# Input projection of a gated convolution block: thirteen seven-product duals and four plain gate blocks in place of twelve duals and eight plain blocks

## The chip, the cores and the metric

The kernel runs on one core of one Trainium2 chip. The core has a matrix engine (TensorE, "PE" in the profile), VectorE (DVE), ScalarE (ACT), GpSimd (POOL), SyncE (SP, which here only issues transfers) and 16 DMA engines. Each engine works through its own list of instructions in order and waits on semaphores for the others. The metric is device time of one execution in microseconds (us).

## The reference

One layer over a sequence of 1024 positions with 1024 channels, in float32 (here cut to the mixing half):

```
h    = rms_norm(x, norm_mix_g) * (1 + sc1) + sh1          # sc1, sh1 from silu(c) @ w_ada + b_ada
proj = h @ w_in                                           # 1024 -> 7 * 1024
b_s, c_s, v_s, v_c, gl_c, gate_a, gate_b = split(proj)
y_a  = (b_s * causal_dwconv3(c_s * v_s)) @ w_short_out
u    = causal_dwconv31(v_c * sigmoid(gl_c)) + bias
y_b  = silu(layer_norm(u)) @ w_conf_out
x    = x + g1 * ((sigmoid(gate_a) * y_a + sigmoid(gate_b) * y_b) @ w_o)
```

Behind it come a second norm, a SwiGLU of width 2816 and a final norm. The change is in `proj = h @ w_in` alone.

## The kernel before

**Layout and precision.** Activations lie transposed: 128 channels on the partitions, positions along the free axis, in two halves of 512. The 1024 channels of h are eight chunks, k = 0 to 7. w_in has 56 output blocks of 128 channels. Each float32 product is made of three matmuls on rounded operands (`mm3`, lines 380 to 383): weights high times x high, weights high times x low, weights low times x high. `split_w` makes the two weight parts: a cast on ScalarE (`wh`, line 226) and a difference on VectorE or GpSimd (`wl`, line 227). There are five raw weight buffers (`raw`), three `wh` and three `wl`; a raw buffer is free for the next load once its split or its matmul is through, and a `wl` once its product is.

**The stages.** The projection runs in three parts.

1. *The lead* (`row_blocks`, called twice): seven blocks at once, one PSUM bank each, chunk by chunk, first for the first half of the positions, then for the second. The activations come to be during it: for each chunk of the first half VectorE reduces two loads of w_ada against silu(c) (`modulation`, line 361), scales x (line 462), splits the weights, and with ScalarE makes the high and low part of h (`modulate`, lines 470 and 471). The first three chunks use whole float32 weights (line 376). In chunk 6 TensorE also sums the squares of the second half (`sum_x1`), from which its norm follows. The seven blocks are three pairs (gl, v) for the long convolution, whose gated product u VectorE makes at the end (`glu`, line 560), and one gate block.
2. *A plain block* (`col_block`): one gate block, both halves, 48 matmuls.
3. *Twelve duals.* A dual takes four output blocks as two pairs, and the matrix of 2 x 2 (upper and lower four chunks by first and second half of the positions) is multiplied with seven products instead of eight, in the order `PRODUCTS = "1265734"`. A product is two pairs times four chunks times three matmuls: 24. The sums of activations that products 6, 5, 7 and 4 need are made once, in VectorE, after the lead. The sums of weights are made per dual on GpSimd (`dual_units`, lines 246 to 251 and 293), which makes `wl` for the duals too. Product 1 goes to bank x, which ScalarE copies to bank y; product 2 is added to y, and 6, 7 and 4 to x; 5 and 3 go to bank z. `win_evac` takes each result out.

**What sets the order.** The program is written in one order, and a planner then lays out each engine's list, by its own estimate of durations and by when a buffer comes free; `tc.issue_after` pins some instructions behind others. `next_w` keeps weights two products ahead. Beside the duals VectorE works off the 31-tap convolution in 46 taps for each channel block (line 915); `CONV_DUALS` spreads the eight blocks over the first eleven duals, each tap pinned behind an evacuation (`read_at`).

## Time and profile before

| | us |
|---|---|
| median of 3 runs (lowest, highest) | 1471.91 (1470.99, 1473.99) |
| the profiled execution | 1470.4 |
| its span, first to last instruction | 1468.6 |
| TensorE busy, share of the span | 1457.7, 99% |
| VectorE busy | 1179.1, 80% |
| ScalarE busy | 615.4, 42% |
| GpSimd busy | 515.8, 35% |

In the rows that follow the first two numbers of a timeline row are the start and the length in us; then come engine, source line, operation, what is written and read, the shape, the count, and in brackets the idle time before and what ended it. "L381" is line 381 of the kernel before. A busy matmul overlaps the next one, so the pace of TensorE is read from the distance of starts. The lead runs from 16.15 to about 97 us, the plain block to about 108, the duals to about 565.

### The profile page before, as it was taken

The page shows a single profiled execution, that of the slowest core. Times are in us where ns is not written, and L with a number is a line of the kernel's source. Part 1 is how long each engine was busy: PE and PEld are TensorE (multiplying, and loading weights), DVE is VectorE, ACT ScalarE, POOL GpSimd, SP SyncE. Part 2 cuts the span into 40 slices and gives each one's busy share as a digit, 9 for nine tenths or more (in the row PEclk, how much of TensorE's full clock was granted, in tenths as well). Part 3 has the DMA queues.
Part 4 walks back from the last instruction along what each step waited for, and adds up shares of the span by engine and source line. Part 5 has one row for each costly group of instructions (what it writes and reads, how often), then busy time and mean ns, then how long its engine had stood idle before and what let it go on. Part 6 is the DMA issues. An engine that isn't in the chain of part 4 may idle for free.

```text
span 1468.6 us, 17760 instructions
## 1 busy us (share of the span) xinstructions
PE 1457.7 (99%) x6443; PEld 1197.3 (82%) x6443; DVE 1179.1 (80%) x1627; ACT 615.4 (42%) x895; POOL 515.8 (35%) x464
## 2 busy tenths in 40 slices
PE   9999999999999999999999999999999999999997
PEld 5888888888888888888888888888888888888887
DVE  8999898887998969999688799776777665676755
ACT  4753333333433346455235475343444443222325
POOL 0046677767777771111022002110111015435005
PEclk9999999999999999999999999999999999999999
DMA  9412313222322258375586337655554449988403
GB/s 369 177 52 72 101 60 127 72 86 101 101 70 76 95 205 300 115 251 206 195 313 219 105 109 236 227 172 166 178 170 170 149 155 373 345 285 275 144 15 115
DMA packets 83913, 247.97 MB, mean 169 GB/s; under 512 B 9665, under 2 KB 11713, under 8 KB 83826
## 3 DMA queue, kind: packets, MB, share of 16 engines
q1 hardware_dynamic: 43072, 138.63, 27.5%
q0 software_dynamic: 37008, 95.63, 19.6%
q10 hardware_dynamic: 3746, 12.59, 2.3%
q8 instruction: 50, 0.82, 0.2%
q14 instruction: 37, 0.30, 0.1%
HBM read 184.41 MB, written 62.39 MB: 168 GB/s over the span
## 4 chain that ended last, share of the span: by engine, by line
PE 97%; DVE 1%; POOL 0%; issue 0%; ACT 0%; POOLq 0%; DVEq 0%
PE bank L380 12%; PE bank L383 12%; PE bank L381 12%; PE x L381 8%; PE x L383 8%; PE x L380 8%; PE z L381 4%; PE z L380 4%; PE z L383 4%; PE y L380 3%; PE y L381 3%; PE y L383 3%; PE mix L383 2%; PE yb L383 2%; PE yb L380 2%; PE mix L381 2%
## 5 line engine op out<-in xcount | busy, mean ns | idle before, releaser
L226 ACT CAST wh<-raw 128x1024 fp32r<-128x1024 f32 (+2 forms) x253 | 255.6, 1011 | 467.6 <-PE bank L381 126.8
L227 POOL TENSOR_TENSOR wl<-raw,wh 128x1024 fp32r<-128x1024 f32 x84 | 204.8, 2446 | 82.1 <-ACT wh L226 82.1
L227 DVE TENSOR_TENSOR wl<-raw,wh 128x1024 fp32r<-128x1024 f32 (+2 forms) x169 | 193.7, 1146 | 37.9 <-ACT wh L226 36.7
L915 DVE SCALAR_TENSOR_TENSOR c<-diff,vec,c 128x512 f32<-128x512 f32 x232 | 171.0, 753 | 4.4
L1263 POOL DMA_DIRECT2D hid<-stage x71 | 37.9, 534 | 346.0 <-DVE stage L421 341.5
L380 PE MATMUL bank<-th,wh 128*128 128x512 f32 x288 | 112.0, 389 | 0.0
L381 PE MATMUL bank<-tl,wh 128*128 128x512 f32 x288 | 112.0, 389 | 0.0
L383 PE MATMUL bank<-th,wl 128*128 128x512 f32 x288 | 112.0, 389 | 0.0
L915 DVE SCALAR_TENSOR_TENSOR c<-u,wsum,c 128x512 f32<-128x512 f32 x112 | 84.3, 753 | 2.6
L246 POOL TENSOR_TENSOR raw<-raw 128x1024 f32<-128x1024 f32 x12 | 29.2, 2431 | 124.1 <-DVE wl L227 86.9
L420 ACT CAST stage<-g 128x512 fp32r<-128x512 f32 x62 | 38.4, 622 | 72.8 <-DMA hid<-stage 39.6
L421 DVE TENSOR_TENSOR stage<-g,stage 128x512 fp32r<-128x512 f32 x62 | 42.5, 689 | 27.5 <-ACT stage L420 27.4
L383 PEld LDWEIGHTS bank<-th,wl 128*128 128x128 f32 x288 | 54.1, 188 | 11.3
L381 PEld LDWEIGHTS bank<-tl,wh 128*128 128x128 f32 x288 | 54.1, 188 | 11.2
L380 PEld LDWEIGHTS bank<-th,wh 128*128 128x128 f32 x288 | 54.1, 188 | 11.2
L1289 POOL DMA_DIRECT2D th<-hid x71 | 38.1, 537 | 53.6 <-PE x L383 32.7
L380 PE MATMUL x<-th,wh 128*128 128x512 f32 x144 | 56.1, 390 | 0.1
L383 PE MATMUL x<-th,wl 128*128 128x512 f32 x144 | 56.0, 389 | 0.0
L381 PE MATMUL x<-tl,wh 128*128 128x512 f32 x144 | 56.0, 389 | 0.0
L246 DVE TENSOR_TENSOR raw<-raw 128x1024 f32<-128x1024 f32 (+1 forms) x17 | 19.2, 1130 | 40.1 <-DMA raw<-in_w_fi 29.0
L380 PE MATMUL yb<-zsh,wh 128*128 128x512 f32 x128 | 49.8, 389 | 0.0
L381 PE MATMUL yb<-zsl,wh 128*128 128x512 f32 x128 | 49.8, 389 | 0.0
(812 smaller groups left out, 4243.2 us busy)
## 6 DMA issues: line engine op xcount, KB each, us to landing
hid<-stage POOLq DMA_DIRECT2D x71, 512.0 KB, 4.6
raw<-in_w_fi SPq DMA_DIRECT2D x54, 512.0 KB, 4.5
raw<-in_w_duals SPq DMA_DIRECT2D x48, 512.0 KB, 3.5
th<-hid POOLq DMA_DIRECT2D x71, 256.0 KB, 5.6
tl<-hid POOLq DMA_DIRECT2D x71, 256.0 KB, 5.6
ada<-in_ada SPq DMA_DIRECT2D x24, 512.0 KB, 5.9
raw<-in_ada SPq DMA_DIRECT2D x24, 512.0 KB, 4.8
raw<-in_w_fo SPq DMA_DIRECT2D x24, 384.0 KB, 5.8
```

Of the source, the lines that this page charges most:

```text
L226: hi = nc.scalar.copy(wh, raw)
L227: lo = lo_engine.tensor_tensor(wl, raw, f32(wh), ALU.subtract)
L246: eng.tensor_tensor(a["s1"], a["21"], a["22"], ALU.add)
L380: nc.tensor.matmul(ps, wh, xh, start=first, stop=False, skip_group_check=again)
L381: nc.tensor.matmul(ps, wh, xl, start=False, stop=False, skip_group_check=again)
L383: mm3.ins = nc.tensor.matmul(ps, wl, xh, start=False, stop=last, skip_group_check=again).ins
L420: t_split.act = nc.scalar.copy(hi, src).ins
L421: t_split.ins = nc.vector.tensor_tensor(lo, src, f32(hi), ALU.subtract).ins
L915: tap.ins = nc.vector.scalar_tensor_tensor(out=out, in0=src[:, s : s + H], scalar=wt, in1=acc, op0=ALU.mult, op1=ALU.add).ins
L1263: nc.gpsimd.dma_start(hid_dram[key], s)
L1289: nc.gpsimd.dma_start(t, hid_dram[key][:, s])
```

## The change

- The lead's seven blocks are now three gate blocks and the four blocks of the two first duals (v and gl of u0 and u1, c and v of p0 and p1). For the latter the lead's first half makes products 1 and 2 of both duals: after four chunks the bank holds product 1, ScalarE copies it to SBUF (`half_way`, into `m1`), and the other four chunks add product 2 to the same bank. The second half makes only the three gate blocks, with splits of 384 columns in place of 896.
- The plain block is the fourth gate block. There are 26 pairs, so thirteen duals; the GLU is made by `win_evac` in all eight cases, and `glu` goes.
- After the plain block come products 1 and 2 of dual 2, then the other five products of duals 0, 1 and 2, then ten duals of seven products (`win_order`). For duals 0 and 1 ScalarE copies product 1 from `m1` into bank x before product 6.
- Duals 0 to 2 use `apart_units`, which loads a block when a product needs it (a second load of block 22 in each). VectorE makes the splits of products 1 and 2 of dual 2 and all of product 6 of dual 0, two sums and a split; GpSimd the rest.
- The sums of activations for products 7 and 4 move behind the plain block in the text. The taps are spread from dual 1.0 over 11.2 duals. `CLOCK` has four filling matmuls in place of five in one place.

```diff
 LEAD = 7
+GATES = 3
+BEGUN = 2
-CLOCK = (10, 3, (5,), 9, 5)
+CLOCK = (10, 3, (5,), 9, 4)
...
-CONV_DUALS = 11
+CONV_FROM, CONV_DUALS = 1.0, 11.2
...
-    def apart_units(mats, eng):
+    def apart_units(mats, eng, on_eng=PRODUCTS):
         def add(out, x, y):
-            eng.tensor_tensor(out, x, y, ALU.add)
+            unit.eng.tensor_tensor(out, x, y, ALU.add)
...
         def unit(m):
+            unit.eng = eng if m in on_eng else nc.gpsimd
             if m in "12":
                 raw = get("1" + m)
...
-            return split_w(raw, 1024, (), eng)
+            return split_w(raw, 1024, (), unit.eng)
...
-    for d in range(len(PAIRS) // 2):
-        units = dual_units([w_duals[d, m] for m in range(4)], 1024, eng=nc.gpsimd)
-        plan += [units[m] for m in PRODUCTS]
+    n_duals = len(PAIRS) // 2
+    win_units = [apart_units([w_duals[d, m] for m in range(4)], nc.vector, "126"[: 3 if d == 0 else 2]) for d in range(BEGUN + 1)]
+    win_units += [dual_units([w_duals[d, m] for m in range(4)], 1024, eng=nc.gpsimd) for d in range(BEGUN + 1, n_duals)]
+    win_order = [(BEGUN, m) for m in "12"] + [(d, m) for d in range(BEGUN + 1) for m in PRODUCTS[2:]]
+    win_order += [(d, m) for d in range(BEGUN + 1, n_duals) for m in PRODUCTS]
+    plan += [win_units[d][m] for d, m in win_order]
...
-                        mm3([outs[o]], slice(o * P, o * P + P), w, [xs], kk == 0, kk == KC - 1)
+                        mm3([outs[o]], slice(o * P, o * P + P), w, [xs], kk == 0, kk == KC - 1 or half and kk == KH - 1, half and kk >= KH)
+                    if half and kk == KH - 1:
+                        half_way(o - whole, outs[o])
...
+    plan[:KC] = [lambda k=k: weights(w_first[k][:, : GATES * P], GATES * P, [modulate.ins[0]]) for k in SECOND[KEPT:]]
+    win_banks = [{} for _ in range(BEGUN)]
+    begun = [win_evac(d, PAIRS[2 * d : 2 * d + 2], win_banks[d]) for d in range(BEGUN)]
+    m1 = [diffp.tile([P, T + CK - 1], F32, tag="diff", name="m1"), uc_tile("m1")]
+    m1 = [t[:, s] for t in m1 for s in halves]
+
+    def half_way(i, ps):
+        nc.scalar.copy(m1[i], ps)
...
+        lead = row_blocks(act_x if h == 0 else lambda i: act_x(SECOND[i], 1), GATES if h else LEAD, "lead", ops,
+                          again_w if h else lead_w, 1 + h, None if h else half_way, GATES)
...
+        for j, ps in enumerate(lead):
+            if j < GATES:
+                gate("b", j, h, ps)
+            else:
+                begun[(j - GATES) // 2]((j - GATES) % 2, "2", ps)
...
+    for banks, x in zip(win_banks, range(BEGUN)):
+        banks.update({(b, p): ring[i][p] for b, i in (("x", x), ("z", 1 - x)) for p in range(2)})
+    win_banks.append({(b, p): ring[i][p] for b, i in (("x", 2), ("y", 1), ("z", 0)) for p in range(2)})
...
+    for d, m in win_order:
+        if d < BEGUN and m == PRODUCTS[2]:
+            for p in range(2):
+                nc.scalar.copy(win_banks[d]["x", p], m1[2 * d + p])
+        product(win_banks[d], m, th[m], win_evacs[d], onto="2")
```

## Prediction

> **What bounds the kernel now.** I read the page first, then the waits and the timelines of TensorE, SyncE, VectorE and GpSimd over the first 200 us, where the change lies. The page, then TensorE's waits and its timeline (start, length, engine, line):

> ```profile
> span 1468.6 us, 17760 instructions
> PE 1457.7 (99%) x6443; PEld 1197.3 (82%) x6443; DVE 1179.1 (80%) x1627; ACT 615.4 (42%) x895; POOL 515.8 (35%) x464
> PE 97%; DVE 1%; POOL 0%; issue 0%; ACT 0%; POOLq 0%; DVEq 0%
> ...
> PE clock L573 <- DVE ones_r L591: 1.6, 1, 1.6
> PE x L381 <- DVE t4l L421: 0.5, 1, 0.5
> PE clock L573 <- DVE newton L635: 0.4, 1, 0.4
> ```
> ```profile
> 16.15 18.18 PE L376 MATMUL lead<-x,raw 128*128 128x512 f32 x42
> 38.95 0.39 PE L380 MATMUL lead<-h40h,wh 128*128 128x512 f32 x1
> 43.71 0.39 PE L380 MATMUL lead<-h50h,wh 128*128 128x512 f32 x1
> 54.81 0.39 PE L381 MATMUL lead<-h70l,wh 128*128 128x512 f32 x1
> 58.89 0.39 PE L380 MATMUL lead<-h51h,wh 128*128 128x512 f32 x1
> 118.73 0.39 PE L380 MATMUL bank<-t2h,wh 128*128 128x512 f32 x1
> 156.81 0.39 PE L380 MATMUL bank<-t2h,wh 128*128 128x512 f32 x1
> ```

> TensorE is the chain: all its shown waits come to 2.5 us, none in the input projection. From chunk 4 to chunk 5 are 21 matmuls in 4.76 us, 0.2267 us each; the 389 ns of a group overlap. A product of 24 is 5.44 us, a dual of seven 38.08 us (118.73 to 156.81). So a matmul that goes is worth 0.2267 us, and idle TensorE time that comes is lost whole. The profiled execution took 1470.4 us, 1.8 around its span and 1.5 under the median of 1471.9.

> Now who is barely ahead of TensorE. VectorE's rows at chunks 4 to 7, then SyncE's queue:

> ```profile
> 32.70 0.74 DVE L471 SCALAR_TENSOR_TENSOR h40l<-x,mod,h40h 128x512 fp32r<-128x512 f32 x1
> 37.64 0.75 DVE L471 SCALAR_TENSOR_TENSOR h50l<-x,mod,h50h 128x512 fp32r<-128x512 f32 x1
> 42.57 0.74 DVE L471 SCALAR_TENSOR_TENSOR h60l<-x,mod,h60h 128x512 fp32r<-128x512 f32 x1
> 49.22 1.28 DVE L361 CUSTOM_DVE_ANT_0 ada<-ada,cs,vec 128x1024 f32<-128x1024 f32 x1
> 53.49 0.74 DVE L471 SCALAR_TENSOR_TENSOR h70l<-x,mod,h70h 128x512 fp32r<-128x512 f32 x1
> ...
> 73.62 0.74 DVE L471 SCALAR_TENSOR_TENSOR h41l<-x,mod,h41h 128x512 fp32r<-128x512 f32 x1
> ```
> ```profile
> 19.74 1.49 SPq L356 DMA_DIRECT2D ada<-in_ada  x2
> 21.27 1.14 SPq L212 DMA_DIRECT2D raw<-in_w_first  x1
> 22.51 1.98 SPq L356 DMA_DIRECT2D ada<-in_ada  x2
> 24.59 0.41 SPq L212 DMA_DIRECT2D raw<-in_w_first  x1
> 25.18 1.50 SPq L356 DMA_DIRECT2D ada<-in_ada  x2
> 28.36 0.33 SPq L212 DMA_DIRECT2D raw<-in_w_first  x1
> ```

> VectorE needs 4.94 us a chunk against TensorE's 4.76, and with the eight squares before chunk 7 it ends h70l at 54.23; TensorE uses it at 54.81. Its lead of 5.5 us at chunk 4 is used up. And the load at 28.36 (chunk 6) waits for its raw slot until TensorE is through chunk 1, which is 16.15 + 2/3 of 18.18 = 28.27: that wait is real on this chip.

> **The change part by part.**

> *Matmuls.* Ten plain half-blocks of 24 for the lead instead of fourteen, 87 products instead of 84: 24 matmuls fewer in the built program, 24 × 0.2267 = 5.4 us off the path. One filling matmul fewer ahead of the lead is at most another 0.23, taken as 0, since the lead also waits there for x.

> *Order of the loads.* In the built program of the changed kernel SyncE's queue reads after chunk 3:

> ```
> raw chunk 4 | raw chunk 5 [PE: chunk 0 done] | raw chunk 6 [PE: chunk 1 done] |
> raw second half [DVE: wl chunk 3] | raw chunk 7 [PE: last matmul of chunk 2] |
> ada chunk 4 x2 | ada 5 x2 | ada 6, ada 6 [DVE] | ada 7 x2 [DVE] | x second half x8
> ```

> The modulation loads of chunk 4 went out at 19.74; now they are behind the raw load of chunk 7, which has to wait for chunk 2, 16.15 + 18.18 = 34.33 us. Two issues later, at about 34.8, ada goes out. How long it takes:

> ```profile
> raw<-in_w_duals SPq DMA_DIRECT2D x48, 512.0 KB, 3.5
> ...
> DMA to landing us min/median/max: 3.4/7.2/10.0
> ```

> The second row is the ada loads of this stage, in a queue that is full; by 34.8 the new queue is empty but for the raw load ahead, so I am nearest to 3.5 and take 4.4: it lands at 39.2 (3.4 gives 38.2, 7.2 gives 42.0). From there one cadence of 4.94 to the end of h40l: 44.1, where it was 33.4. Then what it was: h40l to h70l 20.8 us, so 64.9. Twenty matmuls follow: first half over at 69.6 instead of 58.89, **+10.7** (9.7 to 13.5). TensorE will sit still before chunk 4 (38.95 to about 43) and before the sum of squares, which waits in its queue after six matmuls of chunk 6 (55.5 to 60.2). The half-way copies cost ScalarE four times 0.57, but in its order they stand ahead of h40h, which by then is later anyway: nothing more.

> *Second half, gates alone.* 72 matmuls, 16.3 us, instead of 38.1: VectorE and ScalarE lose that cover. Their rows:

> ```profile
> 60.69 0.73 ACT L470 ACTIVATE h71h<-x,mod 128x512 fp32r<-128x512 f32 x1
> 111.17 0.57 ACT L797 COPY bank<-bank 128x512 f32<-128x512 f32 x1 [0.40 <-ACT sig L564]
> ```
> ```profile
> 75.97 0.69 DVE L718 TENSOR_TENSOR x<-x,x 128x512 f32<-128x512 f32 x1
> 76.57 0.68 DVE L425 SCALAR_TENSOR_TENSOR x<-t,x 128x512 f32<-128x512 f32 x1
> 88.50 1.22 DVE L227 TENSOR_TENSOR wl<-raw,wh 128x1024 fp32r<-128x1024 f32 x1
> 89.65 3.49 DVE L421 TENSOR_TENSOR tl<-x,th 128x512 fp32r<-128x512 f32 x2
> ```

> In the old trace VectorE needs 20.1 us from the end of h70l (54.23) to the end of h41l (74.36). The new list drops three GLU products (0.6 each) and one difference, and has five splits of 384 columns (about 0.5 each by width) for two of 896: 18 us. But ScalarE's list now has x61, a sigmoid and four evacuation copies between h61l and h71h. VectorE ends h61l ten instructions after h70l, 6.7 us, at 71.6; with 0.7, 0.5, 4 × 0.57 and 0.7 h71h ends at 75.8, some 3 us after VectorE could use it. So h41l comes at 64.9 + 18 + 3, about 86.2. Ten matmuls still follow: 88.5, where unhindered it were 69.6 + 16.3 = 85.9: **+2.6** (0 if ScalarE's copies slip between, 4 if the late loads of h51 and h61 add).

> *Dual 0, product 6.* The plain block and products 1 and 2 of dual 2 take 96 matmuls, 21.8 us, to 110.3. Product 6 may start only when ScalarE has put P1 back into the bank, and that copy stands in ScalarE's list behind a split that waits for VectorE's tl of chunk 2. Up to it VectorE has, from h41l on, fifteen instructions of 0.6, four splits and two weight sums of 1.15 now made on VectorE, and five instructions at the pace of the row at 89.65, 1.75 each, since GpSimd works beside them (0.68 without): 24.7 us, to 110.9. Then 0.6 and 0.57: 112.1, **+1.8** (0 to 3).

> *Duals 0 and 1 on GpSimd.* GpSimd's operations and the wait that it meets once in every dual:

> ```profile
> 130.76 2.40 POOL L227 TENSOR_TENSOR wl<-raw,wh 128x1024 fp32r<-128x1024 f32 x1 [3.02 <-ACT wh L226]
> 136.72 2.40 POOL L246 TENSOR_TENSOR raw<-raw 128x1024 f32<-128x1024 f32 x1 [3.56 <-DMA raw<-in_w_duals]
> 139.20 2.40 POOL L249 TENSOR_TENSOR raw<-raw 128x1024 f32<-128x1024 f32 x1
> ...
> POOL raw L246 <- DMA raw<-in_w_duals: 37.2, 11, 3.7
> ```

> A wl frees its raw slot, SyncE loads the next block into it, GpSimd goes on 3.56 us after its wl ended; in a dual of 38.08 us TensorE does not notice. Of duals 0 to 2 only five products are left, 27.2 us, with the same four weight sums (in duals 1 and 2 all on GpSimd), and with five raw slots the sum that needs a block now stands directly behind the wl that frees its slot. The order on GpSimd, "|" where it waits for such a load:

> ```
> wl 7(d0) | s1 s2 s7(d1) wl 4(d0) | s3(d1) wl 6 wl 5(d1) | s1(d2) wl 7(d1) | s7(d2) wl 3(d1) s2(d2) | s3(d2) wl 4(d1)
> ```

> (wl 3 of dual 0 falls into the first gap.) That is 14 × 2.41 + 5 × 3.56 = 51.5 us from wl 7 of dual 0 to wl 4 of dual 1. TensorE does these seven products in 38.1. The first wl waits behind two memsets of tot for VectorE's last tl: nine of 0.6 after chunk 2's, so about 116.9, and ends at 119.4; TensorE wants it at its third matmul of product 7, 112.1 + 10.9 + 0.5 = 123.5. Of the excess 13.4, 4.1 are covered: **+9.3**, met at products 6, 3 and last 4 of dual 1. If all gaps were covered, 33.7 us would do and it costs 0; with no head start it is 13.4.

> *From dual 3 on* the order is the old one, with seven products; the taps end 0.8 of a dual (30 us) before the projection's end, not one, and behind them VectorE sat idle, so nothing:

> ```profile
> 539.96 1.94 DVE L875 TENSOR_TENSOR q<-q,q 128x512 f32<-128x512 f32 x3 [12.70 <-DMA q<-q]
> ```

> *The clock after a standstill.* Rows of the start:

> ```profile
> 1.62 4.63 PE L573 MATMUL clock<-ones_r 128*128 128x512 f32 x10 [1.62 <-DVE ones_r L591]
> 11.67 2.64 PE L573 MATMUL clock<-ones_r 128*128 128x512 f32 x9
> ```

> The first ten matmuls after idle took 4.63 us, 2.4 more than ten at 0.2267. I expect three standstills over 4 us: before chunk 4 (hidden behind VectorE), before the sum of squares, and before product 4 of dual 1. The trace has no idle in mid-run; I take 2.4 for one of the last two, the other being partly hidden by the wait for h70l (0 to 4.8). [...]

> *Sum:* −5.4 + 10.7 + 2.6 + 1.8 + 9.3 + 2.4 = +21.4. On the profiled 1470.4 that is 1491.8; the median stands 1.5 higher: **1493 us**. Nothing behind gives it back, since TensorE is the chain there too.

> **The rivals.** (1) *GpSimd's chain is covered:* loads land while it does other sums, as if slots came back one operation earlier. Speaks for it: the old order hid a gap in each dual. Against: the order puts the sum next to the wl that frees its slot. −9.3 and no cold start there: about 1483. (2) *Every standstill brings the slow clock and the ada loads take their 7.2 us:* 2.8 more for the loads, 2.4 more for the clock, some of each at the smaller gaps: 1498 to 1503. (3) *The loads are not held:* the slot waits bind less than the list says. Place: the raw load of chunk 7 and the five of duals 0 and 1. It decides once ada for chunk 4 lands before 33 us and GpSimd's gaps are under 1.5 us. Then 10.7, 9.3 and the clock go, and if the 4.4 left is covered too only −5.4 stays: 1466.5. Against it is the row at 28.36, which shows the same kind of wait to the tenth of a microsecond, and eleven gaps of at most 3.7. With the 4.4 it is 1471, no change. That matmuls do not fall is excluded by the list.

> **How the numbers follow.** Forecast 0.65, rival 1 0.13, rival 2 0.12, rival 3 0.10 (0.07 of it faster, 0.03 within 0.2%, which is about what a measurement of this kernel can tell from none). Slower: 0.90. The range goes from 1480, rival 1 with the second half and the copies at their low ends, to 1503, rival 2; the forecast's own is 1486 to 1499.

> **What would show it.** In the new profile: 24 matmuls fewer; the first ada load after chunk 3 issued near 34.8; TensorE idle some 4 us before h40h and again before ss, released by VectorE or ScalarE; the second half starting near 69.6 and lasting 19; GpSimd waiting five times about 3.5 us for raw between 116 and 171; TensorE waiting for wl in dual 1; dual 3 seven-product pace of 38.08 unchanged. I am wrong if the built order's waits release earlier than listed, if VectorE is not the pace of chunks 4 to 7, or if the later duals wait as well.

## The result and the profile after

| | median us | range | ratio to before, 95% interval |
|---|---|---|---|
| before | 1472.20 | 1470.99 to 1473.99 | |
| after | 1493.83 | 1493.21 to 1494.77 | 1.0146 (1.0129 to 1.0164) |

The medians are of four executions each. The change costs 1.5%. The forecast was 1493 us in a range from 1480 to 1503, slower with 0.90. The profiled execution of the changed kernel took 1494.3 us.

First the page of the changed kernel, then TensorE's waits (line, what it waited for, us in total, times, longest):

```profile
span 1492.5 us, 17754 instructions
PE 1460.9 (98%) x6418; PEld 1195.5 (80%) x6418; DVE 1179.6 (79%) x1636; ACT 622.0 (42%) x911; POOL 522.9 (35%) x466
PE 79%; issue 4%; POOL 2%; DMA 2%; DVE 2%; ACT 0%; POOLq 0%; DVEq 0%; ACTq 0%
```
```profile
PE bank L389 <- POOL wl L229: 8.1, 3, 5.0
PE lead L386 <- ACT h40h L476: 4.6, 1, 4.6
PE ss L549 <- DVE sq L538: 3.9, 1, 3.9
PE bank L386 <- ACT bank L1009: 2.1, 1, 2.1
PE bank L389 <- DVE wl L229: 0.7, 1, 0.7
```

TensorE has less to do, 6418 recorded matmuls where there were 6443, but its share of the chain falls from 97% to 79%. The first four rows are four places, and they are the four of the forecast. TensorE's timeline (start, length, engine, line; in brackets the idle time before) shows what each place costs:

```profile
43.62 0.90 PE L386 MATMUL lead<-h40h,wh 128*128 128x512 f32 x2 [4.60 <-ACT h40h L476]
60.47 1.44 PE L549 MATMUL ss<-sq,ones 128*128 128x512 f32 x2 [3.86 <-DVE sq L538]
71.19 0.39 PE L386 MATMUL lead<-h51h,wh 128*128 128x512 f32 x1
99.97 0.39 PE L386 MATMUL bank<-h00h,wh 128*128 128x512 f32 x1
113.11 0.50 PE L386 MATMUL bank<-t2h,wh 128*128 128x512 f32 x1 [2.10 <-ACT bank L1009]
160.94 0.50 PE L389 MATMUL bank<-h41h,wl 128*128 128x512 f32 x1 [2.43 <-POOL wl L229]
171.64 0.80 PE L389 MATMUL bank<-th,wl 128*128 128x512 f32 x1 [4.97 <-POOL wl L229]
172.23 0.63 PE L386 MATMUL bank<-th,wh 128*128 128x512 f32 x1
179.31 0.39 PE L386 MATMUL bank<-t2h,wh 128*128 128x512 f32 x1
206.51 0.39 PE L386 MATMUL bank<-h00h,wh 128*128 128x512 f32 x1
```

These rows cut the projection into five stages. A matmul that waits for nothing takes 0.2267 us, so each stage has a floor:

| stage | from, to | floor us | after us | lost | forecast |
|---|---|---|---|---|---|
| first half of the lead | start to 71.19 (before: 58.89) | 58.9 | 71.2 | 12.3 | 10.7 and a part of the clock |
| second half and plain block, 120 matmuls | 71.19 to 99.97 | 27.2 | 28.8 | 1.6 | 2.6 |
| products 1 and 2 of dual 2, 48 | 99.97 to 113.11 | 10.9 | 13.1 | 2.3 | 1.8 |
| product 6 of dual 0 to product 6 of dual 2, 240 | 113.11 to 179.31 | 54.4 | 66.2 | 11.8 | 9.3 and the rest of the clock |
| rest of dual 2 | 179.31 to 206.51 | 27.2 | 27.2 | 0 | 0 |

The losses add up to 27.9 us before rounding. Less the 24 matmuls, 5.4, that makes 22.5. From 206.51 on there are ten duals to go, as there are from 184.01 in the kernel before, and the two marks lie 22.5 apart, so nothing is missing. The spans lie 23.9 apart: in the later y_a stage the changed kernel meets the wait of 0.7 for a split on VectorE.

Why each place is late is in the lists of the other engines. SyncE's queue, then ScalarE and VectorE:

```profile
19.30 15.29 SPq L214 DMA_DIRECT2D raw<-in_w_first  x6
34.64 11.40 SPq L362 DMA_DIRECT2D ada<-in_ada  x8
```
```profile
37.01 1.95 ACT L821 COPY m<-lead 128x512 f32<-128x512 f32 x3 [6.67 <-PE lead L389]
42.85 0.72 ACT L476 ACTIVATE h40h<-x,mod 128x512 fp32r<-128x512 f32 x1 [2.56 <-DVE mod L367]
```
```profile
39.06 1.28 DVE L367 CUSTOM_DVE_ANT_0 ada<-ada,cs,vec 128x1024 f32<-128x1024 f32 x1 [10.31 <-DMA ada<-in_ada]
```

The modulation loads go out at 34.64, behind six raw loads, as the built list said (34.8 was forecast), and VectorE stands still for 10.31 us for them. The row at 37.01 will matter below: ScalarE too had stood still, 6.67 us, for TensorE to end chunk 3. GpSimd between dual 0 and dual 1:

```profile
117.89 4.75 POOL L229 TENSOR_TENSOR wl<-raw,wh 128x1024 fp32r<-128x1024 f32 x2
137.08 2.39 POOL L306 TENSOR_TENSOR raw<-raw 128x1024 f32<-128x1024 f32 x1 [3.66 <-DMA raw<-in_w_duals]
147.78 2.41 POOL L306 TENSOR_TENSOR raw<-raw 128x1024 f32<-128x1024 f32 x1 [3.62 <-PE bank L389]
156.17 2.41 POOL L306 TENSOR_TENSOR raw<-raw 128x1024 f32<-128x1024 f32 x1 [3.62 <-DMA raw<-in_w_duals]
166.95 2.34 POOL L306 TENSOR_TENSOR raw<-raw 128x1024 f32<-128x1024 f32 x1 [3.59 <-DMA raw<-in_w_duals]
169.25 6.98 POOL L229 TENSOR_TENSOR wl<-raw,wh 128x1024 fp32r<-128x1024 f32 x3
```

Each of the four in the middle is a sum that waits some 3.6 us for a block whose slot the operation before it has just freed. (This holds for the one put down to a matmul, too: SyncE issues its load at 144.18, where the operation before it ends.)

### The profile page after: what moved, and what is told of

Its sections match the earlier page's. It is cut to its first block, busy times and chain, and to the rows that moved or that the text cites. A ratio compares the mean times of both kernels' runs of the same rounds, so it can differ in the third digit from the quotient of the medians.

```text
span 1492.5 us, 17754 instructions
## 1 busy us (share of the span) xinstructions
PE 1460.9 (98%) x6418; PEld 1195.5 (80%) x6418; DVE 1179.6 (79%) x1636; ACT 622.0 (42%) x911; POOL 522.9 (35%) x466
## 3 DMA queue, kind: packets, MB, share of 16 engines
q1 hardware_dynamic: 44368, 142.04, 27.9%
## 4 chain that ended last, share of the span: by engine, by line
PE 79%; issue 4%; POOL 2%; DMA 2%; DVE 2%; ACT 0%; POOLq 0%; DVEq 0%; ACTq 0%
PE bank L389 10%; PE bank L386 10%; PE bank L387 10%; PE x L387 7%; PE x L389 7%; PE x L386 7%; PE z L386 3%; PE z L387 3%; PE z L389 3%; PE y L387 3%; PE y L389 3%; PE y L386 3%; PE mix L389 2%; PE mix L386 2%; PE yb L386 2%
## 5 line engine op out<-in xcount | busy, mean ns | idle before, releaser
L228 ACT CAST wh<-raw 128x1024 fp32r<-128x1024 f32 (+3 forms) x256 | 256.2, 1002 | 462.3 <-PE bank L387 135.9
L229 DVE TENSOR_TENSOR wl<-raw,wh 128x1024 fp32r<-128x1024 f32 (+3 forms) x172 | 196.1, 1140 | 37.2 <-ACT wh L228 36.1
L938 DVE SCALAR_TENSOR_TENSOR c<-diff,vec,c 128x512 f32<-128x512 f32 x232 | 168.0, 749 | 2.7
L389 PE MATMUL bank<-th,wl 128*128 128x512 f32 x312 | 122.6, 393 | 5.0 <-POOL wl L229 5.0
L386 PE MATMUL bank<-th,wh 128*128 128x512 f32 x312 | 122.3, 392 | 0.0
L387 PE MATMUL bank<-tl,wh 128*128 128x512 f32 x312 | 122.3, 392 | 0.0
L389 PEld LDWEIGHTS bank<-th,wl 128*128 128x128 f32 x312 | 59.2, 190 | 17.8 <-POOL wl L229 5.4
L426 ACT CAST stage<-g 128x512 fp32r<-128x512 f32 x62 | 38.3, 622 | 76.4 <-DMA hid<-stage 38.1
L386 PEld LDWEIGHTS bank<-th,wh 128*128 128x128 f32 x312 | 59.3, 190 | 12.3
L387 PEld LDWEIGHTS bank<-tl,wh 128*128 128x128 f32 x312 | 59.1, 190 | 12.4
L1317 POOL DMA_DIRECT2D th<-hid x71 | 38.1, 537 | 51.8 <-PE x L389 36.0
## 6 DMA issues: line engine op xcount, KB each, us to landing
hid<-stage POOLq DMA_DIRECT2D x71, 512.0 KB, 4.6
raw<-in_w_duals SPq DMA_DIRECT2D x57, 512.0 KB, 3.5
raw<-in_w_fi SPq DMA_DIRECT2D x54, 512.0 KB, 4.0
ada<-in_ada SPq DMA_DIRECT2D x24, 512.0 KB, 5.4
raw<-in_ada SPq DMA_DIRECT2D x24, 512.0 KB, 4.8
```

Of the source, the lines that this page charges most:

```text
L228: hi = nc.scalar.copy(wh, raw)
L229: lo = lo_engine.tensor_tensor(wl, raw, f32(wh), ALU.subtract)
L386: nc.tensor.matmul(ps, wh, xh, start=first, stop=False, skip_group_check=again)
L387: nc.tensor.matmul(ps, wh, xl, start=False, stop=False, skip_group_check=again)
L389: mm3.ins = nc.tensor.matmul(ps, wl, xh, start=False, stop=last, skip_group_check=again).ins
L426: t_split.act = nc.scalar.copy(hi, src).ins
```

## The experiments

The table has the stages of all of them, in the order above, from the starts of the same matmuls in each TensorE timeline. "Start" is where the second half starts; the others are lengths.

| kernel | median us | start | second half and plain block | products 1, 2 | dual 0 to dual 2 | rest of dual 2 |
|---|---|---|---|---|---|---|
| floor | | 58.9 | 27.2 | 10.9 | 54.4 | 27.2 |
| after | 1493.8 | 71.2 | 28.8 | 13.1 | 66.2 | 27.2 |
| e1 load order | 1492.2 | 70.3 | 27.8 | 13.2 | 65.3 | 27.2 |
| e2a two more slots | 1482.6 | 73.5 | 28.8 | 13.2 | 54.6 | 27.4 |
| e2b product 6 on VectorE | 1489.8 | 70.9 | 29.1 | 13.1 | 62.0 | 27.2 |
| e4 warm | 1492.5 | 69.6 | 30.0 | 13.2 | 64.3 | 27.2 |
| e5 order and copies | 1484.9 | 62.2 | 30.0 | 13.2 | 65.8 | 27.2 |
| e7 and slots | 1473.4 | 60.4 | 29.9 | 13.2 | 54.5 | 27.8 |
| e8 copies placed | 1475.5 | 61.6 | 31.5 | 10.9 | 55.8 | 31.2 |
| e9 P1 copy | 1470.1 | 60.8 | 30.0 | 10.9 | 55.1 | 27.2 |
| e10 splits on GpSimd | 1472.2 | 61.4 | 31.6 | 10.9 | 54.6 | 27.2 |
| e11 made late | 1470.0 | 60.6 | 29.6 | 11.1 | 54.4 | 27.2 |

The first matmul of the lead starts between 15.9 and 16.1 in most of these profiles, at 16.9 in e5, e8 and e10 and at 18.4 in e2a: "start" can be off by that much. The kernel before, run again beside the experiments, had medians from 1471.8 to 1472.8, so a difference of about 1 us between kernels of different rows can come from when they were run.

**The loads (e1).** The raw load of a chunk is issued behind the modulation loads of the same chunk.

```
-            nc.sync.dma_start(raw, ada[i])
+            modulation.ins = nc.sync.dma_start(raw, ada[i]).ins
...
-        w = weights(w_first[k], LEAD * P, modulate.ins[:1])
+        with tc.issue_after(modulation.ins):
+            w = weights(w_first[k], LEAD * P, modulate.ins[:1])
```

> Each raw load of the lead's weights from chunk 3 on is put behind the two modulation loads of its own chunk in SyncE's queue; nothing else changes. Theory (the loads were held behind the raw load of chunk 7): the first ada load of chunk 4 goes out before 25 us, TensorE no longer stands still before h40h and ss, the second half starts near 59 to 60 in place of 71.2, and the kernel takes 1481.5 us (1480 to 1484) against 1493.8. Rival (VectorE and ScalarE would pace these chunks anyway, since ScalarE now makes four half-way copies): the ada loads go out early, but the second half starts at 65 or later, 1487 or more.

1492.2 us: the theory misses by 11, although the loads go out as wanted. SyncE and ScalarE of e1:

```profile
20.94 1.53 SPq L362 DMA_DIRECT2D ada<-in_ada  x2
```
```profile
36.96 2.62 ACT L822 COPY m<-lead 128x512 f32<-128x512 f32 x4 [7.87 <-PE lead L389]
40.32 0.72 ACT L476 ACTIVATE h40h<-x,mod 128x512 fp32r<-128x512 f32 x1
```

The loads of chunk 4 go out at 20.94, 13.7 us earlier, and h40h comes only 2.5 earlier. ScalarE stands for 7.87 us at the first half-way copy, which reads what TensorE has to finish in chunk 3; the weight split of chunk 4 and h40h are queued behind it. The rival has the late start (70.3) and names the half-way copies, but took the work of VectorE and ScalarE for the pace. The row shows a wait, not work, and VectorE was no pace either: it stood still for 8.7 us for that split.

**The loads and the copies (e5).** As e1, and chunks 4 and 5 are prepared before the copies. The loads of the x halves also move behind the modulation loads of chunk 7, the raw load of chunk 7 behind those, and the second half's weight loads behind the last of the first half. The two edits that matter most:

```
+                while half_way and k == KH - 1 and len(ops) <= k + MADE:      # MADE = 2
+                    xs = act(len(ops))
+                    ops.append((unit(len(ops)), xs))
...
     def half_way(i, ps):
-        nc.scalar.copy(m1[i], ps)
+        with tc.issue_after(modulate.ins[1]):                                 # behind h50h
+            nc.scalar.copy(m1[i], ps)
```

> The loads in the order of e1, and ScalarE's four half-way copies behind h50h instead of ahead of the weight split of chunk 4 (chunks 4 and 5 are prepared before them; the loads of the x halves move behind the modulation loads of chunk 7, and the raw load of chunk 7 behind those). New theory, from the trace of e1: two things held chunk 4, each alone enough for most of it, the loads (h40h at 42.85) and the copies, which ScalarE can only make when TensorE is through chunk 3 (h40h at 40.32 in e1). With both gone TensorE has no wait before h40h, the second half starts near 59.5 and the kernel takes 1482 us (1480 to 1484) against 1493.8. Rival (VectorE is the pace in any case): TensorE still waits for h40h or ss for more than 3 us in all, 1487 or more.

1484.9 us, 8.9 less than the changed kernel where the loads alone gave 1.6. ScalarE of e5, then TensorE:

```profile
33.43 0.72 ACT L477 ACTIVATE h40h<-x,mod 128x512 fp32r<-128x512 f32 x1 [1.47 <-DVE x L469]
38.99 1.54 ACT L836 COPY m<-lead 128x512 f32<-128x512 f32 x3
```
```profile
52.73 1.10 PE L553 MATMUL ss<-sq,ones 128*128 128x512 f32 x2 [1.90 <-DVE sq L542]
62.24 0.39 PE L387 MATMUL lead<-h51h,wh 128*128 128x512 f32 x1
```

h40h is at 33.43 and TensorE has no wait there. Two holds stood side by side, and taking one away shows the other. It is 2.9 short of its 1482: the start is 0.9 later in this profile, the squares of the second half of x are 1.9 late (ScalarE starts them at 45.95, directly behind an instruction that waited for h60l), and the second half now loses 2.8 and not 1.6.

**GpSimd's chain (e2a, e2b).** e2a gives two blocks of dual 1 a slot in the pool of the wide tiles; the work stays, but the planner lays out GpSimd's list a little differently. e2b moves three operations of dual 1 and leaves the slots.

```
e2a  -            return load(mats[...])
     +            return load(mats[...], 1024, uc_tile if m + b in spare else None)   # spare = ("611", "312") in dual 1
e2b  -    "126"[: 3 if d == 0 else 2]
     +    "126"[: 3 if d < 2 else 2]
```

> Two weight blocks of dual 1 (11 for product 6, 12 for product 3) are loaded into slots of another pool, so that GpSimd's sums find their block loaded; the work of every engine is the same. From the built order three of the five waits of 3.56 us between product 7 of dual 0 and product 4 of dual 1 go or are covered by a wl of 2.41: the chain is 39.6 us in place of 51.5, under the 42.2 that TensorE has. Theory (waits for slots and GpSimd's work add up): TensorE's waits for wl in dual 1 (1.1, 2.7 and 5.0) go but for 1 us, and with them the slow clock: 1482 us (1481 to 1485). Rival (GpSimd's work alone is too much, the waits are cover): within 2 us of 1493.8.

> Product 6 of dual 1 has its two sums and its split on VectorE, as dual 0 has; three operations of 2.41 us leave GpSimd and all five waits for slots stay. Theory (waits and work add up): the chain is 44.3 us in place of 51.5, some 2 us over TensorE's 42.2, each standstill is below 3.4 us and the clock stays full: 1484 us (1483 to 1487). Rival (the loads alone set the pace): within 2 us of 1493.8. Rival (VectorE pays for it, being late itself): 1488 or more, with TensorE waiting for VectorE.

e2a: 1482.6 us, as the theory had it, and the stage falls to 54.6, its floor but for 0.2. GpSimd of e2a between product 7 of dual 0 and product 4 of dual 1:

```profile
126.23 7.25 POOL L306 TENSOR_TENSOR raw<-raw 128x1024 f32<-128x1024 f32 x3 [1.26 <-issue]
137.21 2.41 POOL L306 TENSOR_TENSOR raw<-raw 128x1024 f32<-128x1024 f32 x1 [1.36 <-DMA raw<-in_w_duals]
150.19 4.92 POOL L306 TENSOR_TENSOR raw<-raw 128x1024 f32<-128x1024 f32 x2 [3.51 <-issue]
```

The gap of 1.26 is not new: the changed kernel has 1.20 at this place. Of its four gaps of 3.6 one is down to 1.36, one of 3.51 is left, and two are gone from this stretch, with the same operations. From the end of product 7's split of dual 0 (122.6) to the end of product 4's split of dual 1 (162.2) GpSimd takes 39.6 us, as the theory had it, where the changed kernel takes 51.3. So the waits for slots are what is too much; the work alone fits. e2b gave 4.0 of the 9.8 expected. Its GpSimd and TensorE:

```profile
125.18 3.44 POOL L306 TENSOR_TENSOR raw<-raw 128x1024 f32<-128x1024 f32 x1 [1.24 <-DVE raw L306]
144.00 2.40 POOL L306 TENSOR_TENSOR raw<-raw 128x1024 f32<-128x1024 f32 x1 [3.75 <-issue]
```
```profile
168.40 0.50 PE L389 MATMUL bank<-th,wl 128*128 128x512 f32 x1 [3.89 <-POOL wl L229]
```

TensorE's last wait ends at 168.40, 3.2 earlier than the 171.64 of the changed kernel, where 7.2 was expected: GpSimd now waits for VectorE's sum, its own sum beside VectorE takes 3.44 in place of 2.41, and the slot gaps stay. TensorE's standstill there is still 3.9, and slow matmuls follow it, where the theory had each standstill below 3.4 and the clock full. No run shows 3.4 us to be such a bound: in these traces 8 of the 14 standstills from 1.90 to 2.51 us have slow matmuls behind them (last section). The time lies in the range of the second rival, but TensorE waits for GpSimd and not, as that rival has it, for VectorE.

**The clock (e4).** Eighteen matmuls by zero fill the standstill ahead of product 4 of dual 1. (A filler tile gives up the space for the zero block.)

```
+            for _ in range(warm):                         # warm = 18 in product 4 of dual 1
+                nc.tensor.matmul(ps, zero, xh, start=False, stop=False, skip_group_check=again)
```

> The changed kernel with 18 matmuls by a zero weight block put into product 4 of dual 1, behind its first two and ahead of the first that needs wl, where TensorE stood still for 5.0 us; they add zero to the sum. Everything else stays, the wait for GpSimd too. Theory (a standstill of about 5 us costs the clock): the matmuls behind it run at 0.2267 us from the first on, and the time falls by 2.4 to 2.9: 1491.0 us. Rival (these matmuls are slow because of something beside them, such as GpSimd or the loads): pitch still 0.427, 1493.8 or 1494.

1492.5 us, half of the gain. TensorE of e4 at that place, with the wait that came 11 us earlier:

```profile
160.60 0.57 PE L393 MATMUL bank<-h41h,wl 128*128 128x512 f32 x1 [2.04 <-POOL wl L231]
160.97 0.63 PE L388 MATMUL bank<-h51h,wh 128*128 128x512 f32 x1
161.40 0.63 PE L389 MATMUL bank<-h51l,wh 128*128 128x512 f32 x1
167.77 4.36 PE L391 MATMUL bank<-th,zero 128*128 128x512 f32 x18
171.97 0.39 PE L393 MATMUL bank<-th,wl 128*128 128x512 f32 x1
176.99 0.39 PE L388 MATMUL bank<-t2h,wh 128*128 128x512 f32 x1
```

From the first matmul that needs wl to product 6 of dual 2 are 22 matmuls: 5.02 us here (171.97 to 176.99), 7.67 in the changed kernel (171.64 to 179.31). So the standstill's slow clock costs 2.65, and work in its place removes it. The same stretch in both kernels, changed kernel first (from, to, length, TensorE's busy time and matmuls, granted clock as a share of the full one, busy share of the DMA engines, GB/s):

```profile
172.20:176.00 3.80, 3.80 (x10) 0.50 0.61 224
```
```profile
172.20:176.00 3.80, 3.80 (x18) 1.00 0.80 251
```

The rival falls with these rows: the loads move more bytes beside the matmuls in e4, GpSimd makes the same splits, and the matmuls run at full pace. Dual 3 starts 2.3 earlier; 1.2 of that is lost again in a later dual, which takes 39.2 us in place of 38.1 because a split on GpSimd comes 0.8 late. The slow matmuls after a standstill of only 2.04 were not foreseen; more on them below.

**Both places (e7)** is e5 with the slots of e2a.

> e5 together with the two slots of e2a. If the lead and the duals are separate places on the path, the gains add: 1482 less the 11.3 of e2a, 1470.7 us (1469 to 1473). Rival (the lead's earlier end only brings TensorE sooner to a GpSimd chain that starts late, for it begins with VectorE's splits): TensorE waits for wl in dual 1 again, 1475 or more.

1473.4 us. From e5 that is 11.5 less, and e2a alone gave 11.3: the two places are separate and add. The rival falls; TensorE's wait for GpSimd there is 0.3.

**The smaller terms (e8, e9).** e8 places two sets of ScalarE copies:

```
-            for i in range(2))]                             # operands of the second half made ahead: 3, with h71h
+            for i in range(3))]
...
+                with tc.issue_after(modulate.ins[1]):
                     begun[(j - GATES) // 2]((j - GATES) % 2, "2", ps)
...
-        if d < BEGUN and m == PRODUCTS[2]:                  # copies of P1 of dual 0: ahead of product 2 of dual 2
+        if (d, m) in ((BEGUN, "2"), (1, PRODUCTS[2])):
```

> e7, with the copies of the four begun products to u0, u1, p0 and p1 behind h71h, and the two copies of P1 of dual 0 into its bank traced ahead of product 2 of dual 2 (two splits earlier in ScalarE's list). Theory (these were the 1.6 of the second half and the 2.1 ahead of product 6): 2 to 3.5 less than e7, 1468 us (1466.5 to 1470), below the kernel before. Rival (VectorE is as late as ScalarE at both places): within 1 us of e7.

> e7 with the copies of P1 of dual 0 traced ahead of product 2 of dual 2 (the trace of e8 shows product 6 of dual 0 without a wait then), and the sums of product 3 of duals 1 and 2 behind the splits of product 7 on GpSimd, so that a wait for a slot no longer stands ahead of the split of product 6; ScalarE's evacuation copies are where the changed kernel has them. From the built order GpSimd needs 38.5 us from product 7 of dual 0 to product 6 of dual 2, where TensorE has 43.5. Theory (the 2.1 us ahead of product 6 and the 0.6 behind dual 1 are on the path): e7 less 2.7, 1470.7 us (1469 to 1472.5). Rival (GpSimd takes over as the one that is late, as in e8): 1473 or more, with TensorE waiting for wl.

e8 is 2.1 slower than e7. Its P1 copy works: the stage is 10.9, with no wait ahead of product 6. But with the weights of one chunk more fetched ahead ScalarE waits for a slot of wh:

```profile
67.88 0.51 ACT L229 CAST wh<-raw 128x384 fp32r<-128x384 f32 x1 [1.17 <-PE lead L388]
```

and the second half with the plain block takes 31.5. GpSimd then is late again behind dual 1: TensorE waits 2.07 at 162.47, nine slow matmuls follow, and the rest of dual 2 takes 31.2 where 27.2 is the floor. e9 keeps the P1 copy, drops the other edit and puts the sum of product 3 behind the split of product 7 on GpSimd: 1470.1 us, 3.3 less than e7 (2.7 expected), 0.9993 of the kernel before (0.9984 to 1.0002), no difference that can be told.

**What is left of the second half (e10, e11).** e10 gives its weight splits to GpSimd (`lo_engine=nc.gpsimd`) and moves the x loads forward; e11 makes the four evacuation copies only behind the second half:

```
-            else:
-                begun[(j - GATES) // 2]((j - GATES) % 2, "2", ps)
...
+    for j, ps in enumerate(made):                          # made = the first half's lead[GATES:]
+        begun[j // 2](j % 2, "2", ps)
```

> e9 with two more edits in the lead: the loads of the x halves ahead of the modulation loads of chunk 7, and the five splits of the second half's weights on GpSimd, which is idle there, in place of VectorE (5 times 0.55). Theory (the second half, 72 matmuls or 16.3 us, took 19.0 in e7 because VectorE and ScalarE have more to do than that): it takes 17 us or less, and ss loses its wait of 0.9: 2.5 to 3.5 less than e9, 1467.5 us (1466 to 1470), below the kernel before. Rival (ScalarE alone is the pace of the second half, as e8 suggests): the second half still takes 18.5 or more, within 1.5 us of e9.

> e9 with the evacuation of the four begun products (u0, u1, p0, p1, four copies of 0.57 us on ScalarE) traced behind the second half instead of ahead of it, so that h71h stands ahead of them; the weight splits stay on VectorE. Theory (these copies are what VectorE waits 2.3 us for at h71l, and ScalarE is dense from there to h41h): the second half takes 17 us in place of 19.1 and the kernel 2 us less than e9, 1468 us (1467 to 1470), faster than before by 0.2 to 0.3%. Rival (VectorE's own work is the pace of the second half, the wait only moves): the second half still takes over 18.3, within 1 us of e9.

e10: 1472.2 us, and second half and plain block take 1.6 longer than in e9. The second half is over 18.5, as the rival has it, but the kernel is 2.1 slower than e9, which neither foresaw. The same VectorE instruction in e9 and in e10, and GpSimd of e10 beside it:

```profile
73.48 0.75 DVE L479 SCALAR_TENSOR_TENSOR h21l<-x,mod,h21h 128x512 fp32r<-128x512 f32 x1
```
```profile
73.57 1.49 DVE L479 SCALAR_TENSOR_TENSOR h21l<-x,mod,h21h 128x512 fp32r<-128x512 f32 x1
```
```profile
73.29 1.22 POOL L230 TENSOR_TENSOR wl<-raw,wh 128x384 fp32r<-128x384 f32 x1 [0.98 <-ACT wh L229]
```

VectorE saves 0.55 for the split and pays 0.74 at the instruction beside it. Over the stage it saves 2.75 for five splits, and the five instructions that run beside them on GpSimd take 3.0 more than in e9.

e11: 1470.0 us, 0.9988 of the kernel before (0.9979 to 0.9997) and 0.1 us from e9, which is no difference. h71h comes earlier, yet the stage falls by 0.4 only (30.0 to 29.6), and the second half still takes 18.7, as the rival had it. VectorE's wait of 2.34 at h71l comes back as three, of 0.37, 0.58 and 0.68. These lie beside a wait of ScalarE, 0.82 at 65.28, for a slot of wh that TensorE frees, the hold that e8 met too; so VectorE's own work is not the whole reason, and how much of the stage is work stays open.

## Why the prediction was right, and where its steps were not

The total holds: 1493 forecast, 1493.8 measured; of rival 1 (GpSimd covered, 1483), rival 2 (1498 to 1503) and rival 3 (loads not held, 1466.5) none came. That the two agree to 0.8 us is in part luck. The profiled executions lie 23.9 apart, where 21.4 was forecast; but the profile before happened to lie 1.8 under the 1472.2 of the median, and the profile after 0.5 over its own. Point by point:

*Matmuls, −5.4.* Right: the stage losses less 5.4 give the measured shift of 22.5. e9 adds up in the same way: it loses 1.9, 2.8, 0 and 0.7 in its stages, 5.3 before rounding, and its dual 3 starts at 183.90 where the kernel before is at 184.01.

*Order of the loads, +10.7.* Right in size and place, wrong as a single cause. The first half loses 12.3; about 1.2 of that are slow matmuls behind the sum of squares, from which to the second half the changed kernel takes 10.72 us and e4, without them, 9.51. The ada issue at 34.64 and the 39.06 where VectorE takes the first load are the forecast's 34.8 and 39.2. The failing sentence is the one on the half-way copies, "nothing more". Under the late loads they do cost nothing more, but they hold chunk 4 nearly as long by themselves (h40h 42.85 in the changed kernel, 40.32 in e1, 33.43 in e5). The order of the loads is worth 1.6 us alone, little more than what medians of one kernel differ by; with the copies it is worth 8.9. Whether the copies moved alone would give anything was not tried, since moving them draws the loads of chunks 4 and 5 forward too.

*Second half, +2.6.* 1.6 in the changed kernel, 2.7 to 2.8 in e4, e5, e7 and e9. The forecast has it from 69.6 to 88.5. In e4, where no slow matmuls follow the sum of squares, it runs from 69.56 to 88.66; in the changed kernel it starts 1.6 later and ends at 89.10. So its end is set by VectorE and ScalarE and hardly by its start, and the term is right. Its working has a slip: 64.9 + 18 + 3 is 85.9 and not 86.2, which would make it 2.3. The cause named, ScalarE's copies ahead of h71h, is in the trace (h71h ended at 75.84, 75.8 was forecast):

```profile
75.09 0.75 ACT L476 ACTIVATE h71h<-x,mod 128x512 fp32r<-128x512 f32 x1
```

but e11 shows that it carries 0.4 of it; the rest lies in the work of VectorE and ScalarE for 72 matmuls and in the next waits behind it, and how it divides is open.

*Dual 0, product 6, +1.8.* 2.3, and e8 and e9 take it away by tracing the copy earlier.

*Duals 0 and 1 on GpSimd, +9.3.* TensorE lost 9.1 there without the clock: 11.8 less the 2.65; 8.1 of it are its waits for wl. From the end of product 7's split of dual 0 (the first of the pair at 117.89, so 120.3) to the end of product 4's split of dual 1 (the first of the three at 169.25, so 171.6) GpSimd took 51.3; 51.5 was added up from 14 operations and five waits. (The first of the five holds wl 3 of dual 0 and 1.20 of waiting.) e2a shows that the waits decide it. Its mirror, e2b, was mis-sized because three operations moved away made GpSimd wait for VectorE.

*The clock, +2.4.* Right to 0.3, one place in full and the other hidden, though for the most part not by the wait for h70l that the prediction names. Behind product 4 the slow clock costs 2.65 (e4). Behind the sum of squares the granted clock is 0.50 from 61.10 to 64.51, too, and the second half starts the later for it. What hides it is VectorE's pace: e4 has no slow matmuls there, so it meets a short wait for h70l (0.24 us, at 64.90) and starts the second half 1.6 earlier, but ends the plain block only 0.4 earlier (99.53 for 99.97), and 0.4 it was ahead already at the sum of squares (60.05 for 60.47). On the path one place cost 2.65 and the other next to nothing.

*Not forecast:* 1.4 us between dual 3 and the end of the span, with the wait of 0.7 in the y_a stage. It stays open why; e1 and e5 have a wait of the same kind, e2a, e7 and e9 do not.

## What to carry to other kernels

When a stage is late, list everything that stands ahead of its first instruction on every engine: a second hold under the first costs nothing until the first is mended, and then it is nearly the whole cost. With an engine that sums in place and shares a few load slots, count the wait between freeing a slot and having it filled (3.6 us here) as work; two more slots gave 11 us here, where moving a fifth of the work gave 4. And a change that shortens a matmul stage takes away the cover of all that ran beside it, even where the matmuls saved are real: the 5.4 us saved here come out as less than 2 us in the best version, since its first half still loses 1.7 and its shorter second half 2.4.

## What the runs showed of the hardware

```profile
108.78:112.19 3.41, 1.21 (x6) 1.00 0.65 216
112.19:115.60 3.41, 3.41 (x10) 0.50 0.08 30
```
```profile
108.89:112.30 3.41, 2.13 (x10) 1.00 0.42 154
112.30:115.71 3.41, 2.60 (x11) 1.00 0.50 156
115.71:119.12 3.41, 3.41 (x17) 1.00 0.01 2
```

In e1 the wait falls into one window, which is idle for 2.20 us, and the whole next window is slow. It begins 0.9 us after TensorE has started again, so three matmuls still run at full pace, and the eight or nine slower ones cost 1.6. In the changed kernel the edge of a window cuts the wait into 1.28 and 0.81, and no slow matmul follows. Over all twelve profiles, from the first change of the clock (at 6.49 in the changed kernel) to 1440 us, the same holds: each of the 21 full-clock windows with 1.95 us or more of idle was followed by a slow one, and of 80 with 0.3 to 1.81 us none was. A slow window with 0.63 us or more of idle was followed by another slow one (four cases), with 0.60 or less by the full clock. These bounds are read off the traces that they describe, and no run was made to test them. Less than a whole window of idle was enough: 2.20 us of 3.41 in e1.

Since the windows lie differently in each of these profiles, a wait of about 2 us should be carried with 0 us (as in the changed kernel) to 1.6 us (as in e1) beside its length, an estimate from these two cases. The four executions of the changed kernel had mean granted clocks from 0.990 to 0.994, yet their times lie within 1.6 us and do not follow the clock. A slow window that another engine's pace hides, as behind the sum of squares, would explain that; it was not looked into.
